# A GLA and MLP layer on one core: where prepared weight sums are made, and which steps of the output projection use them

## The chip, the cores and the metric

The kernel runs on one core of one Trainium2 chip. The metric is the device time of one execution in microseconds, the median of the runs shown; lower is better.

## The reference, cut to what matters

One layer with 256 tokens (T) of width 2048 (D): a chunk-causal gated linear attention (GLA) and a squared-ReLU MLP, each behind an RMSNorm and added to the residual, and a last RMSNorm. All is float32.

```python
h = x
h = h + _gla_mixer(_rmsnorm(h, gla_norm[j]), gla_w_in[j], gla_w_gate_up[j], gla_b_gate[j], gla_o_norm[j], gla_w_out[j])
h = h + _sq_relu_mlp(_rmsnorm(h, mlp_norm[i]), mlp_w_up[i], mlp_w_down[i])
return _rmsnorm(h, final_norm)
```

The mixer projects to q and k (1024 wide each), v and r (2048 wide each) and a gate of rank 16, attends in chunks of 64 tokens with 4 heads, normalizes each head, multiplies by silu(r) and projects back to 2048 through `gla_w_out`. The MLP goes through 8192.

## The kernel before, in words

**Splitting.** Each float32 operand is split into a high part (`hi`, rounded to fp32r by a ScalarE copy, line 123) and the rest (`lo`, a VectorE subtraction, lines 136 and 170). A product is three matmuls: high by high, low by high, high by low. Each matmul here has 128 rows, a stationary side of 128 columns and a moving side of 256. TensorE (PE) does one after the other; PEld, its weight load, runs beside it.

**Weights.** They come by DMA from SyncE's queue (SP) into one of six `raw` tiles, are split into one of five pairs of slots `hi` and `lo` (`wpool`, `slots`), and a slot is free again when PE has used it. So the loads and the splitting run ahead of PE as far as raw tiles and slots allow.

**Stages, in order of time.** v's first half with the gate (`natural`); k's two halves and then q's two halves (`turned`, 24 matmuls to a pair of k-tiles, line 224); four groups `x_group` 0 to 3 for v's second half and r's first half; r's second half (`natural`, line 181); the output projection as four groups `out_group` 0 to 3 of 512 columns; the MLP (line 1022). While the stages up to the q halves run, `pump` places small jobs of other work between their k-tiles: it takes one from `side` and one from `jobs` after each k-tile, 15 times to a half.

**Groups (`group`, line 305).** A group takes the 8 pairs of k-tiles in a written order. A *plain* pair is 8 blocks of 3 = 24 matmuls. A pair *by sums* (those in `summed`) uses seven products in place of eight, 21 matmuls, on sums and differences of the four blocks of weights and of the four blocks of the other side: 9 matmuls on the weights as they are, in the pair's own step, and 12 on the sums (`pending`), behind the next step's products. The sums are made on the spot: the load adds two blocks by a DMA from GpSimd's queue (POOL, line 335), VectorE does `weight_sums` (lines 233 and 234), ScalarE and VectorE split them again (lines 123 and 365). A step whose place is in `between` has other work behind its products.

**Prepared steps (`make_sums`, `make_all`).** For the pairs in `MADE_OUT`, as (group, pair) of the output projection, the sums are made earlier, by two jobs from `jobs`: `high` loads the weights, adds and subtracts on VectorE (lines 252, 233, 234), rounds on ScalarE (255) into a slot and writes it to HBM from POOL's queue (256); `low` subtracts (259) and writes the rest (260). The slot is held until both writes have landed. `MADE_AT` has the places, one tuple for each call of `next(make)`, a place being the number of the job in that stage. In the group, a prepared pair is loaded ready (`pre<-made`, line 330), so neither adding load, nor sums, nor their splitting is needed; only the 768 columns that the first 9 matmuls read are split.

**Two things around the change.** `xe_gt` holds copies, at another address, of the first 128 tokens of the k-tiles in `EVEN` (5 and 6). `rows_of` names pairs of an `x_group` whose first product reads its stationary side from there (`row_x`); `FIRST[2]` does that for pair 2 and also puts k-tile 5 first, `FIRST[3]` for pair 3. `two_scores` (line 697) does the attention scores of two heads, in float32, in two banks of their own and two that `x_group` 1 will use; ScalarE and VectorE evacuate them to `at` (711, 712). `turn` transposes a piece of h through PE (line 844) behind step 2 of groups 1 to 3, so that it waits for the group before to have been added up (`put`, 933).

**The order of the work.** Each engine's queue is put in order by a planner that runs a timeline of its own over the program, within what `issue_after` fixes; PE's order of products is fixed by `then_mm`. So a job that is moved can change the order on ScalarE, VectorE, POOL and SP around it.

Of the kernel before, what the change touches and what calls it, by code (L numbers as in the profile page):

```python
# [41 lines left out]
KEYW = HEADS * DK  # L42
# [6 lines left out]
GT = 512  # L49
# [20 lines left out]
def tile_gla_mlp(ctx, tc, x, xt, cols, w_vg, w_in, w_gate, w_out, w_up, w_down, final_norm, out):  # L70
# [26 lines left out]
    side, jobs = deque(), deque()  # L97
# [113 lines left out]
    def turned(row, w, c0, even=(0,), acc=None):  # L211

        acc = acc or acc_banks(GT // P // 2)
        for kp in range(KT // 2):
            wh, wl = pair_of(w, kp, c0, even)
            for i in range(2):
                kt = 2 * kp + i
                ah, al = row(kt)
                for j in range(GT // P):
                    s = slice(j * P, (j + 1) * P)  # L220
                    o = acc[j // 2][:, j % 2 * T : (j % 2 + 1) * T]
                    for n, (u, m) in enumerate(((wh, ah), (wh, al), (wl, ah))):

                        nc.tensor.matmul(  # L224
                            o, u[:, i, s], m, start=kt == 0 and n == 0 and j % 2 == 0,
                            stop=kt == KT - 1 and n == 2, skip_group_check=True,
                        )
                if kt < KT - 1:
                    pump()
        return acc  # L230
# [3 lines left out]
        return nc.vector.tensor_tensor(u[:, 1::2], u[:, 1::2], u[:, 2:3].to_broadcast([P, 2, T]), op=ALU.subtract)  # L234


    MADE_OUT = ((1, 6), (2, 1), (2, 6), (3, 1), (3, 6))
    MADE_DOWN = ()
    MADE_AT = ((0, 5, 10), (6, 10))
    made = {}  # L240

    def make_sums(key, src):

        made[key] = dram.tile([2, P, G], F32, tag=f"made{len(made)}", name="made")
        raw, to = [], []

        def high():
            raw.append(raw_tile()[:, :G])
            with tc.issue_after(last_load[0].ins):
                last_load[0] = nc.sync.dma_start(out=raw[0].rearrange("p (i c) -> p i c", i=2), in_=src)  # L250
            u = raw[0].rearrange("p (f s) -> p f s", f=4)
            nc.vector.tensor_tensor(u[:, 0], u[:, 0], u[:, 1], op=ALU.add)
            weight_sums(u)
            to.extend(slots())
            nc.scalar.copy(to[0][:, :G], raw[0])
            nc.gpsimd.dma_start(out=made[key][0], in_=to[0][:, :G].bitcast(F32))

        def low():
            nc.vector.tensor_tensor(to[1][:, :G], raw[0], to[0][:, :G].bitcast(F32), op=ALU.subtract)
            nc.gpsimd.dma_start(out=made[key][1], in_=to[1][:, :G].bitcast(F32))  # L260

        return high, low

    def make_all():
        pair = lambda w, c0, g: w[c0 : c0 + 2 * P, g * GT : (g + 1) * GT].rearrange("(i p) c -> p i c", p=P)
        todo = [make_sums((None, g, kp), pair(w_out, 2 * kp * P, g)) for g, kp in MADE_OUT]
        todo += [make_sums((ROUNDS - 1, g, kp), pair(w_down, (ROUNDS - 1) * MR + 2 * kp * P, g)) for g, kp in MADE_DOWN]
        for places in MADE_AT:
            now = [lambda: None] * (KT - 1)
            for at in places:  # L270
                now[at], now[at + 1] = todo.pop(0)
            yield now
# [155 lines left out]
    def plain_x(kt, t):  # L428
        return x_row(kt, t * P, (t + 1) * P)
# [11 lines left out]
    def from_bank(dst, bank):  # L441

        b = bank.rearrange("p (i t) -> p i t", i=2)
        nc.scalar.copy(dst[:, :, WRAP:T], b[:, :, : T - WRAP])
        nc.vector.tensor_copy(dst[:, :, :WRAP], b[:, :, T - WRAP :])
# [222 lines left out]
    def extend_q(c):  # L668
        nc.scalar.copy(qt[:, c, T : T + CHUNK], qt[:, c, CHUNK:P])
        nc.vector.tensor_tensor(  # L670
            qt[:, c, T + CHUNK :].rearrange("p (b s) -> p b s", b=2),
            qt[:, c, P:T].rearrange("p (b s) -> p b s", b=2),
            dq[:, c, :].unsqueeze(2).to_broadcast([P, 2, CHUNK]),
            op=ALU.mult,
        )

    make = make_all()
    for half in range(2):
        if half:
            jobs.extend(next(make))  # L680
        acc = turned(stream_x, w_in, half * GT, even=())
        for b in range(2):
            c0 = 4 * half + 2 * b
            from_bank(qt[:, c0 : c0 + 2], acc[b])
        side.extend([lambda c=c: extend_q(c) for c in range(4 * half, 4 * half + 4)])
# [41 lines left out]
    def two_scores(hd):  # L727
        spare = [psum_bank(i, "aux") for i in x_banks[1]]
        scores(hd)
        scores(hd + 1, spare)  # L730

    def x_group(n, c0, order, summed, between, put, rows_of={}):

        def combine(p16, p57):
            tt = nc.vector.tensor_tensor
            nc.scalar.copy(comb_x[:, 1::2], two(p16))
            nc.scalar.copy(comb_x[:, 0::2], two(p57))
            tt(comb_x[:, 3], comb_x[:, 1], comb_x[:, 3], op=ALU.add)
            tt(comb_x[:, 0], comb_x[:, 0], comb_x[:, 3], op=ALU.subtract)
            tt(comb_x[:, 3], comb_x[:, 3], comb_x[:, 2], op=ALU.add)  # L740
            tt(comb_x[:, 2], comb_x[:, 0], comb_x[:, 2], op=ALU.subtract)

        def put_all(banks):
            for t in range(NT):
                o = comb_x[:, 2 * t : 2 * t + 2]
                nc.vector.tensor_tensor(o, two(banks[t]), o, op=ALU.add)
                put(o.rearrange("p f s -> p (f s)"), t)

        def at_of(kp):
            def at(k):  # L750
                if k < A12:
                    return [x_forms[kp][:, i, k] for i in range(2)]
                t, i = divmod((A11, A12, A21, A22).index(k), 2)
                return plain_x(2 * kp + i, t)
            return at

        def row(kt, t):
            return (row_x if (kt, t) in [(2 * kp + i, t) for kp in rows_of for t, i in rows_of[kp][:1]] else plain_x)(kt, t)

        group(  # L760
            lambda kp: w_in[2 * kp * P : 2 * (kp + 1) * P, c0 : c0 + GT], [psum_bank(i) for i in x_banks[n % 2]], x_sums,
            order, summed, between, row, at_of, combine, put_all, filled=False, rows_of=rows_of,
        )

    V0 = (5, 0, 6, 2, 4, 3, 7, 1), (0, 4)
    V1 = (2, 5, 0, 3, 4, 6, 1, 7), (0, 4, 1)
    G0 = (2, 5, 0, 3, 4, 6, 1, 7), (0, 4, 1)
    G1 = (2, 0, 5, 4, 3, 1, 6, 7), (0, 4, 1)
    FIRST = {2: ((0, 1), (0, 0), (1, 0), (1, 1)), 3: ((0, 0), (0, 1), (1, 0), (1, 1))}
    rest = [side.popleft() for _ in range(len(side))]  # L770
    at_of_v = lambda c: lambda bank, t: put_v(bank, 512, t, G + c)
    x_group(0, 3 * KEYW, *V0, {
        **{i: lambda i=i: [f() for f in rest[2 * i : 2 * i + 2]] for i in range(2)},
        2: lambda: two_scores(0), 4: lambda: two_scores(2),
    }, at_of_v(0), FIRST)
    x_group(1, 3 * KEYW + GT, *V1, {}, at_of_v(GT))

    on = big.tile([P, NT, D], F32, tag="C", name="on")

# [45 lines left out]
    FORMED = (0, 1, 6, 7)  # L825
# [93 lines left out]
    def out_group(g, order, summed, between):  # L919

        def combine(p16, p57):
            tt = nc.vector.tensor_tensor
            nc.scalar.copy(comb[:, 1:3], two(p16))
            nc.scalar.copy(comb[:, 0:4:3], two(p57))
            tt(comb[:, 2], comb[:, 1], comb[:, 2], op=ALU.add)
            tt(comb[:, 0], comb[:, 0], comb[:, 2], op=ALU.subtract)
            tt(comb[:, 4], comb[:, 0], comb[:, 3], op=ALU.subtract)
            tt(comb[:, 5], comb[:, 2], comb[:, 3], op=ALU.add)

        def put(banks):  # L930
            for t in range(NT):
                o = h[:, t, g * GT : (g + 1) * GT].rearrange("p (f s) -> p f s", f=2)
                nc.vector.tensor_tensor(o, two(banks[t]), comb[:, 4 * t : 4 * t + 2], op=ALU.add)

        def at_of(kp):
            f = forms_o(kp)
            return lambda k: [a[:, k] for a in f]

        group(
            lambda kp: w_out[2 * kp * P : 2 * (kp + 1) * P, g * GT : (g + 1) * GT], [out_banks[g, t] for t in range(NT)], out_ids[4:],  # L940
            order, summed, between, row_o, at_of, combine, put, ready_of=lambda kp: made.get((None, g, kp)),
        )
# [6 lines left out]
    ORDER = (3, 0, 2, 1, 4, 7, 6, 5), (1, 3, 7, 2, 0, 6, 4, 5)  # L949
# [6 lines left out]
    hth, htl = (big.tile([P, KT, T], F32R, tag="A" + i, name="h" + i, bufs=1) for i in "hl")  # L956
    turned_h = lambda kt: [a[:, kt, :].rearrange("p (t s) -> p t s", t=NT) for a in (hth, htl)]
    for g in range(1, GROUPS):
        out_group(g, ORDER[1], FORMED, {
            2: lambda: turn(h, turned_h, g2, g - 1), 4: lambda: ssq_h(g - 1),  # L960
            **({3: lambda: begin_out(g + 1)} if g + 1 < GROUPS else {}),
        })
# [511 lines left out]
```

## Time and profile before

| what | us |
|---|---|
| runs shown | 1046.91, 1046.59, 1043.65 (median 1046.59) |
| the profiled execution | 1045.65 |
| its span, from the first to the last instruction | 1043.9 |
| PE busy | 1032.6 |
| VectorE (DVE) busy | 908.7 |
| ScalarE (ACT) busy | 755.5 |

Times in the trace count from the start of the span. A row of a timeline gives start, duration, engine, line, operation, tiles written and read, count, and in brackets the idle time of the engine just before and what ended it. A row of a window gives, for each engine, its busy time and the number of instructions that touch the window, then the granted clock of TensorE, the busy share of the DMA engines and GB/s. A row of grouped lines gives count, busy time and mean ns of one, and the idle time before. In a busy stretch of PE the matmuls overlap: each shows some 276 ns while the next starts after some 113.

### The profile page before, as it was taken

The page shows a single profiled execution, that of the slowest core. Times are in us where ns is not written, and L with a number is a line of the kernel's source. Part 1 is how long each engine was busy: PE and PEld are TensorE (multiplying, and loading weights), DVE is VectorE, ACT ScalarE, POOL GpSimd, SP SyncE. Part 2 cuts the span into 40 slices and gives each one's busy share as a digit, 9 for nine tenths or more (in the row PEclk, how much of TensorE's full clock was granted, in tenths as well). Part 3 has the DMA queues.
Part 4 walks back from the last instruction along what each step waited for, and adds up shares of the span by engine and source line. Part 5 has one row for each costly group of instructions (what it writes and reads, how often), then busy time and mean ns, then how long its engine had stood idle before and what let it go on. Part 6 is the DMA issues. An engine that isn't in the chain of part 4 may idle for free.

```text
span 1043.9 us, 23395 instructions
## 1 busy us (share of the span) xinstructions
PE 1032.6 (99%) x9013; PEld 1031.0 (99%) x9013; DVE 908.7 (87%) x1261; ACT 755.5 (72%) x1133; POOL 135.0 (13%) x183
## 2 busy tenths in 40 slices
PE   9999999999999999999999999999999999999997
PEld 9999999999999999999999999999999999999997
DVE  7768868898698866889999999999999999999887
ACT  7775456666577665677788788778778778778685
POOL 0000110220100000111111111111111111111000
PEclk9999999999999999999999999999999999999999
DMA  9866786758977987678888888888888888887772
GB/s 336 320 206 197 240 264 177 202 168 288 317 252 224 308 252 190 180 211 223 239 243 218 248 228 219 240 234 223 248 231 216 256 227 228 236 231 221 232 243 86
DMA packets 129615, 242.66 MB, mean 232 GB/s; under 512 B 11568, under 2 KB 30384, under 8 KB 129376
## 3 DMA queue, kind: packets, MB, share of 16 engines
q1 hardware_dynamic: 108048, 216.76, 66.1%
q0 software_dynamic: 20736, 22.82, 12.5%
q8 instruction: 70, 1.15, 0.4%
q10 hardware_dynamic: 720, 1.60, 0.4%
q14 instruction: 41, 0.34, 0.1%
HBM read 233.79 MB, written 7.34 MB: 231 GB/s over the span
## 4 chain that ended last, share of the span: by engine, by line
PE 94%; DVE 2%; DMA 1%; issue 1%; ACT 1%; POOL 0%; POOLq 0%; DVEq 0%; ACTq 0%
PE up L1022 33%; PE acc L1022 28%; PE acc L305 14%; PE acc L181 10%; PE acc L224 5%; PE aux L224 2%; DVE lo L136 1%; DMA made<-hi 1%; PE aux L181 1%; PE aux L844 1%; DMA raw<-in_w_in 0%; ACT hi L123 0%; PE aux L399 0%; PE aux L697 0%; DVE lo L170 0%
## 5 line engine op out<-in xcount | busy, mean ns | idle before, releaser
L123 ACT CAST hi<-raw 128x512 fp32r<-128x512 f32 (+4 forms) x656 | 518.6, 821 | 201.6 <-DVE raw L233 70.8
L136 DVE TENSOR_TENSOR lo<-raw,hi 128x768 fp32r<-128x768 f32 (+4 forms) x228 | 232.7, 1031 | 53.7 <-ACT hi L123 49.4
L1022 PE MATMUL acc<-hi,act 128*128 128x256 f32 x1696 | 247.7, 276 | 0.0
L1022 PE MATMUL up<-hh,hi 128*128 128x256 f32 x1024 | 238.7, 276 | 0.0
L1022 PE MATMUL up<-hl,hi 128*128 128x256 f32 x1024 | 238.7, 276 | 0.0
L1022 PEld LDWEIGHTS acc<-hi,act 128*128 128x128 f32 x1696 | 217.6, 188 | 0.0
L170 DVE TENSOR_TENSOR lo<-raw,hi 128x1024 fp32r<-128x1024 f32 x160 | 194.5, 1219 | 24.9 <-ACT hi L123 23.9
L1022 PEld LDWEIGHTS up<-hh,hi 128*128 128x128 f32 x1024 | 192.2, 188 | 0.0
L1022 PEld LDWEIGHTS up<-hl,hi 128*128 128x128 f32 x1024 | 192.2, 188 | 0.0
L1232 POOL DMA_DIRECT2D raw<-in_w_down x112 | 95.8, 856 | 519.8 <-DMA raw<-in_w_down 259.5
L1292 DVE TENSOR_TENSOR lo<-raw,hi 128x1024 fp32r<-128x1024 f32 x112 | 136.5, 1218 | 1.1 <-ACT hi L123 1.1
L1022 PE MATMUL up<-hh,lo 128*128 128x256 f32 x1024 | 137.0, 276 | 0.0
L1022 PE MATMUL acc<-lo,act 128*128 128x256 f32 x848 | 133.8, 276 | 0.0
L1022 PEld LDWEIGHTS up<-hh,lo 128*128 128x128 f32 x1024 | 125.7, 188 | 0.0
L1022 PEld LDWEIGHTS acc<-lo,act 128*128 128x128 f32 x848 | 113.3, 188 | 0.0
L234 DVE TENSOR_TENSOR raw<-raw 128x512 f32<-128x512 f32 x139 | 96.0, 690 | 3.5
L233 DVE TENSOR_TENSOR raw<-raw 128x256 f32<-128x256 f32 x139 | 58.8, 423 | 7.7 <-DMA raw<-in_w_out 4.7
L181 PE MATMUL acc<-hi,xA 128*128 128x256 f32 (+1 forms) x376 | 56.0, 281 | 0.0
L181 PEld LDWEIGHTS acc<-hi,xA 128*128 128x128 f32 x376 | 49.9, 190 | 0.0
L224 PE MATMUL acc<-xA,hi 128*128 128x256 f32 x288 | 49.2, 276 | 0.0
L224 PEld LDWEIGHTS acc<-xA,hi 128*128 128x128 f32 x288 | 43.4, 188 | 0.0
L1149 ACT COPY sums<-acc 128x512 f32<-128x512 f32 x46 | 26.9, 584 | 22.4 <-PE acc L1022 22.4
(226 smaller groups left out, 1450.7 us busy)
## 6 DMA issues: line engine op xcount, KB each, us to landing
raw<-in_w_up SPq DMA_DIRECT2D x128, 512.0 KB, 4.6
raw<-in_w_down SPq DMA_DIRECT2D x224, 256.0 KB, 4.4
raw<-in_w_in SPq DMA_DIRECT2D x69, 512.0 KB, 4.5
raw<-in_w_down POOLq DMA_DIRECT2D x112, 128.0 KB, 5.1
raw<-in_w_out SPq DMA_DIRECT2D x21, 512.0 KB, 6.4
raw<-in_w_down SPq DMA_DIRECT2D x16, 512.0 KB, 5.0
raw<-in_w_vg SPq DMA_DIRECT2D x14, 520.0 KB, 8.6
raw<-in_w_out SPq DMA_DIRECT2D x27, 256.0 KB, 5.3
```

Source lines behind the costliest of these rows:

```text
L123: last_hi[0] = nc.scalar.copy(to, raw)
L136: last_lo[0] = nc.vector.tensor_tensor(lo[:, s], raw[:, s], hi[:, s].bitcast(F32), op=ALU.subtract)
L170: last_lo[0] = nc.vector.tensor_tensor(to[1], dst, to[0].bitcast(F32), op=ALU.subtract)
L181: newest[0] = nc.tensor.matmul(o[:, m], x, w[:, m], start=first and c == 0, stop=last, skip_group_check=True).ins
L224: nc.tensor.matmul(o, u[:, i, s], m, start=kt == 0 and n == 0 and j % 2 == 0, stop=kt == KT - 1 and n == 2, skip_group_check=True,)
L233: nc.vector.tensor_tensor(u[:, 2], u[:, 0], u[:, 2], op=ALU.subtract)
L234: return nc.vector.tensor_tensor(u[:, 1::2], u[:, 1::2], u[:, 2:3].to_broadcast([P, 2, T]), op=ALU.subtract)
L305: newest[0] = nc.tensor.matmul(bank[:, o + d : o + d + T], x, w[:, d : d + T], start=(not filled or bank in sums_banks) and bank.name not ...
L1022: newest[0] = nc.tensor.matmul(o, x, w, start=first, stop=last, skip_group_check=True).ins
L1149: last_end[0] = nc.scalar.copy(to, src).ins
L1232: nc.gpsimd.dma_start(out=raw[:, :T], in_=src[:, 0, T:], accum_op=ALU.add)
L1292: last_lo[0] = nc.vector.tensor_tensor(to[1][:, :G], u, to[0][:, :G].bitcast(F32), op=ALU.subtract)
```

## The change

Of the output projection's prepared steps, four are left of five: pairs 1 and 6 of group 1 change places, pair 6 of group 2 is not prepared any more, pair 1 of groups 2 and 3 and pair 6 of group 3 are as before. Pair 6 of groups 1 and 2 is plain. One step is prepared in q's first half (places 2 and 3), one in its second half (4 and 5) in place of three; the two in r's second half stay. `x_group` 0 takes its pairs in another order, so that the pairs by sums, 0 and 4, are its fourth and seventh steps and no longer the second and fifth; the first two heads' scores stand behind its second step and no longer its third, the other two behind the fifth as before, and two of the four `extend_q` jobs behind the third and not the second. Pairs 2 and 3, which read `xe_gt`, stay the ones behind the scores. `x_group` 1 gets `FIRST[2]`.

```diff
-    MADE_OUT = ((1, 6), (2, 1), (2, 6), (3, 1), (3, 6))
+    MADE_OUT = ((1, 1), (2, 1), (3, 1), (3, 6))
     MADE_DOWN = ()
-    MADE_AT = ((0, 5, 10), (6, 10))
+    MADE_AT = ((2,), (4,), (6, 10))
...
     for half in range(2):
-        if half:
-            jobs.extend(next(make))
+        jobs.extend(next(make))
         acc = turned(stream_x, w_in, half * GT, even=())
...
-    V0 = (5, 0, 6, 2, 4, 3, 7, 1), (0, 4)
+    V0 = (5, 6, 2, 0, 7, 3, 4, 1), (0, 4)
...
     x_group(0, 3 * KEYW, *V0, {
-        **{i: lambda i=i: [f() for f in rest[2 * i : 2 * i + 2]] for i in range(2)},
-        2: lambda: two_scores(0), 4: lambda: two_scores(2),
+        0: lambda: [f() for f in rest[0:2]], 2: lambda: [f() for f in rest[2:4]],
+        1: lambda: two_scores(0), 4: lambda: two_scores(2),
     }, at_of_v(0), FIRST)
-    x_group(1, 3 * KEYW + GT, *V1, {}, at_of_v(GT))
+    x_group(1, 3 * KEYW + GT, *V1, {}, at_of_v(GT), {2: FIRST[2]})
...
     for g in range(1, GROUPS):
-        out_group(g, ORDER[1], FORMED, {
+        out_group(g, ORDER[1], FORMED if g == 3 else (0, 1, 7), {
             2: lambda: turn(h, turned_h, g2, g - 1), 4: lambda: ssq_h(g - 1),
```

`FORMED` is (0, 1, 6, 7), `ORDER[1]` is (1, 3, 7, 2, 0, 6, 4, 5).

## The prediction

> **What bounds the kernel now.** I read the page first, then PE in windows, then the chain of waits and the timelines around the places where PE loses time.
>
> ```profile
> span 1043.9 us, 23395 instructions
> PE 1032.6 (99%) x9013; PEld 1031.0 (99%) x9013; DVE 908.7 (87%) x1261; ACT 755.5 (72%) x1133; POOL 135.0 (13%) x183
> ```
>
> PE is busy all through. So time comes only from three things: the number of matmuls, the places where PE runs dry, and the distance between matmuls that follow each other. The page hides the third, since ends are modelled; a window shows it, by its count (columns: PE busy us, twice, count, granted clock, DMA share, GB/s):
>
> ```profile
> 161.20:191.20 30.00, 30.00 (x257) 1.00 0.68 181
> 193.00:241.00 48.00, 48.00 (x426) 1.00 0.64 181
> 327.00:339.60 12.60, 12.60 (x110) 1.00 0.97 309
> ```
>
> A window counts what overlaps its edges, so a matmul that shows 276 to 280 ns is counted 2.4 times too often. 254.6 in 30 us is one per 117.8 ns; 423.6 in 48 us is one per 113.3 ns. Both are 128x256 matmuls at clock 1.00. So there are two spacings, 4.5 ns (4%) apart; the third row (117.1) is in the long one. The long spacing starts where PE runs dry and stays. What ended it:
>
> ```profile
> 170.55 0.63 PE L305 MATMUL acc<-hi,xA 128*128 128x256 f32 x4
> ...
> 192.10 0.64 PE L305 MATMUL acc<-hi,xe_gt 128*128 128x256 f32 x4
> 192.58 0.40 PE L305 MATMUL acc<-lo,xe_gt 128*128 128x256 f32 x2
> 192.81 0.62 PE L305 MATMUL acc<-hi,xA 128*128 128x256 f32 x4
> 193.27 0.39 PE L305 MATMUL acc<-lo,xA 128*128 128x256 f32 x2
> ```
>
> The six matmuls whose stationary side is the copy xe_gt (x_group 2's first step, by FIRST[2]) stand between long and short: from 192.81 four take 0.46 us. x_group 1 lies whole in the long spacing: 183 matmuls from 170.55 to 192.10.
>
> **Dry spots in x_group 0.**
>
> ```profile
> 143.74 0.67 PE L305 MATMUL acc<-hi,xE 128*128 128x256 f32 x4
> 144.93 0.50 PE L305 MATMUL acc<-lo,xE 128*128 128x256 f32 x2 [0.52 <-DVE lo L136]
> 145.27 0.63 PE L305 MATMUL acc<-hi,xE 128*128 128x256 f32 x4
> ...
> 148.86 3.25 PE L697 MATMUL aux<-qt,kab 128*128 128x128 f32 x24
> 151.86 0.72 PE L305 MATMUL acc<-hi,xe_gt 128*128 128x256 f32 x4
> ...
> 155.72 0.28 PE L305 MATMUL acc<-lo,xf 128*128 128x256 f32 x1
> 156.39 0.92 PE L697 MATMUL aux<-qt,kab 128*128 128x192 f32 x4 [0.39 <-DVE at L712]
> 158.14 2.67 PE L697 MATMUL aux<-qt,kab 128*128 128x128 f32 x20 [0.83 <-PE aux L697]
> 160.57 0.72 PE L305 MATMUL acc<-hi,xe_gt 128*128 128x256 f32 x4
> ```
>
> At 143.74, six matmuls take 1.53 us where 6 x 0.1133 = 0.68 would do: 0.85 lost. The first scores take 3.00 us (148.86 to 151.86); the second 160.57 - 155.84 = 4.73: 1.73 lost, for the evacuations of the first (`at`, L712). Where the first loss is from:
>
> ```profile
> 134.09 8.41 DMA made<-hi
> ```
>
> ```profile
> 142.57 1.05 ACT L123 CAST hi<-raw 128x1024 fp32r<-128x1024 f32 x1 [7.05 <-DMA made<-hi]
> ```
>
> The third prepared step of the q projection's second half keeps one of five weight slots until its write has landed; ACT sits 7.05 us before it can split step 2's weights, DVE behind it. That backlog is also why the first scores are evacuated so late.
>
> **Dry spots in the output projection.**
>
> ```profile
> 315.87 1.38 PE L844 MATMUL aux<-ident,h 128*128 128x128 f32 x8
> 317.00 0.48 PE L305 MATMUL acc<-hi,oth 128*128 128x256 f32 x2
> ...
> 322.94 0.54 PE L305 MATMUL acc<-lo,oth 128*128 128x256 f32 x3
> 323.71 1.26 PE L305 MATMUL acc<-hi,of 128*128 128x256 f32 x8 [0.24 <-ACT hi L123]
> 325.50 0.74 PE L305 MATMUL acc<-lo,of 128*128 128x256 f32 x4 [0.52 <-DVE lo L365]
> ...
> 326.97 0.40 PE L305 MATMUL acc<-hi,oth 128*128 128x256 f32 x2
> ...
> 339.69 1.03 PE L844 MATMUL aux<-ident,h 128*128 128x128 f32 x8
> 340.49 0.48 PE L305 MATMUL acc<-hi,oth 128*128 128x256 f32 x2
> ```
>
> Group 1's eight transposes take 1.13 us, group 2's 0.80: 0.33 lost, waiting for h. From 322.94 to 326.97 stand 21 matmuls in 4.03 us; 2.38 would do: 1.65 lost, and the long spacing stays until the transposes at 339.69 (12.72 us, 108 matmuls, 0.49 lost). Here VectorE is the cause:
>
> ```profile
> 296.00:309.00 13.00, 13.00 (x116) 13.00 (x115) 12.72 (x17) 8.51 (x12) 0.84 (x1) 1.00 0.82 280
> 309.00:326.00 17.00, 16.12 (x134) 15.47 (x133) 15.18 (x24) 12.97 (x25) 0.86 (x1) 1.00 0.66 196
> ```
>
> ```profile
> L136 DVE TENSOR_TENSOR lo<-raw,hi 128x1024 fp32r<-128x1024 f32 x14 | 16.8, 1221 | 1.3 <-ACT hi L123 1.3
> L136 DVE TENSOR_TENSOR lo<-raw,hi 128x768 fp32r<-128x768 f32 x15 | 14.3, 953 | 0.5 <-ACT hi L123 0.5
> L365 DVE TENSOR_TENSOR lo<-raw,hi 128x1024 fp32r<-128x1024 f32 x11 | 13.4, 1222 | 3.0 <-ACT hi L123 2.9
> L234 DVE TENSOR_TENSOR raw<-raw 128x512 f32<-128x512 f32 x10 | 6.9, 689 | 0.2
> L233 DVE TENSOR_TENSOR raw<-raw 128x256 f32<-128x256 f32 x10 | 4.2, 423 | 3.6 <-DMA raw<-in_w_out 3.6
> ```
>
> In the windows of all engines the columns are PE, PEld, DVE, ACT, POOL: DVE is busy 12.72 of 13, then 15.18 of 17 us. The other rows give the pieces: a step by sums made on the spot costs DVE 0.95 + 0.42 + 0.69 + 1.22 = 3.28 us, a prepared one 0.95, a plain one 1.22.
>
> **The change, part by part.**
>
> (a) Prepared steps in the q halves. Before three in half 1, after one in each half. One costs DVE 0.42 + 0.42 + 0.69 + 1.22 = 2.75 us (L252 taken at the 0.42 of L233, same shape), ACT one 1.05 us cast, SP one load, POOL two writes, and one of five slots. Half 1 loses 5.5 us of DVE work, and its last write is issued six jobs earlier (4 for 10, one job per 12 matmuls: 8.2 us). The 0.85 at 143.74 goes. What is late next: slots stay 4 x 24 x 0.1133 = 10.9 us ahead of PE, less 2.7 for a held one, so ACT and DVE reach x_group 0 with 8 us in hand; the ends are 0 and 0.85.
>
> In half 0 the prepared step is new, and its cover must be looked at:
>
> ```profile
> 85.00:100.00 15.00, 15.00 (x135) 15.00 (x134) 14.09 (x22) 6.99 (x8) 0.00 (x0) 1.00 0.83 243
> 100.00:110.00 10.00, 10.00 (x91) 10.00 (x90) 5.84 (x10) 7.54 (x8) 0.00 (x0) 1.00 0.64 171
> ```
>
> ```profile
> 93.84 1.05 ACT L123 CAST hi<-raw 128x1024 fp32r<-128x1024 f32 x1 [1.67 <-PE acc L224]
> ```
>
> DVE has 0.9 us free in 85 to 100 and 4.2 in 100 to 110. ACT's cast at 93.84 waits for PE to free a slot, so splitting is as far ahead as slots allow: about 8.6 us (10.9 less cast and subtraction, 2.3). A held slot takes 2.7, DVE's added work 2.75: 3 us stay. POOL, which issues the writes, has nothing else there (0.00), and SP's one load meets a DMA share of 0.83, then 0.64. I take nothing; if the cover goes, PE runs dry by what is missing, bounded by the 1.73 above, and the long spacing comes early (rival 3). Below nothing it cannot be: PE is not dry there now.
>
> (b) V0's order. Both lots of scores are still followed by the xe_gt steps (kp 2, kp 3). Between the two lots lie now two plain steps, a first half and a second half of sums: 24 + 9 + 24 + 12 = 69 matmuls, some 8 us, where before were 36 (151.86 to 155.84, 4 us). The evacuation of the first scores, on ACT and DVE among casts, ended near 156.3, 4.4 us after them. I take all of the 1.73; ends 0 and 1.73, nearer to the upper since the ACT backlog goes too. The first scores come a step earlier and share banks with q's half 1; two plain steps (48 matmuls, 5.4 us) still lie between. Two extensions of q run a step later, three steps ahead of the scores that read them. Both xe_gt steps behind scores leave the long spacing as it is (161.20 row); I expect that again. Steps 0 and 1 now run at 113.3 before the scores: some 20 matmuls, 0.1.
>
> (c) V1 with FIRST[2]. Enters as x_group 2 did at 192.10, from the long spacing with the same six matmuls: 177 x 4.5 ns = 0.79 gained; x_group 2's own then costs 6 x 4.5 ns. Ends 0 and 0.82.
>
> By the Trainium skill (TensorE: Matmul & The Clock Gate, Back-to-back issue gap) a warm gap is N/2.4 + 2.5 ns, 109.2 for 256 columns, whatever tile the operand is read from; by it (c) is worth 0. The rows show 113.3 and 117.8 at the same N and clock, so the trace does not agree.
>
> (d) Group 1: pair 1 prepared, 6 plain. DVE loses 3.28 - 0.95 = 2.33 us before the transposes, and gains 0.27 for pair 6. Between pair 0's first half and its sums stand 24 matmuls, not 9: 1.7 us more time. So 3.7 us of slack against 1.65 lost: I take all of 0.33 + 1.65 + 0.49 = 2.47. The ends are 0 and 2.47. PE pays 3 matmuls, 0.34. SP's two reads of a made tile are for pair 1 and not pair 6; POOL has one adding load less:
>
> ```profile
> 292.81 2.41 SPq L330 DMA_DIRECT2D pre<-made x4
> ```
>
> The first two made tiles are read at 292.81 now, as soon as their buffers come free, and would be then, some 20 us ahead of pair 1's sums.
>
> (e) Group 2: 6 plain, not prepared: DVE +0.27, 1 MB less to load, PE 0.34. Groups 0 and 3, the r projection's two prepared steps and the MLP stay as they are.
>
> Sum: 0.85 + 1.73 + 0.10 + 0.79 + 2.47 - 0.68 = 5.26 us. The profiled execution took 1045.65 us for its span of 1043.9; it lies between the runs shown (1043.65 to 1046.91, median 1046.59). 1045.65 - 5.26 = **1040.4**.
>
> **Rivals.** (1) VectorE still late in group 1: (d) gives only its cost, 1045.65 - 3.47 + 0.68 = 1042.9. For it: 12.72 of 13 us busy in group 0, which the change leaves; against: the work that goes lies ahead of the loss. (2) The wait in x_group 0 moves and isn't removed, to the first sums or the scores' banks; the planner orders the queues anew, so the change would not do what it says: 2.68 stays, 1043.1. (3) **Slower**: the prepared step in half 0 makes PE dry. Point: a backlog of over 3 us on DVE or ACT around 100 to 110. Price: 1.7 dry, then the long spacing until 241, where the second window above ends, since the xe_gt steps behind scores have failed twice and V1's and x_group 2's would too: 136 us from 105, less the 47.2 (144.9 to 192.1) that have it now, 88.8 x 4.5/117.8 = 3.4; with (a) and (b) lost because the queues stay late, and (d) and (e) gained (1.79), 1.7 + 3.4 - 1.8 = 3.3 slower, 1049.0. (4) The spacing follows other things than the xe_gt reads: (c), 0.10 and 0.49 go, 1041.8. The skill's rule above would give this.
>
> **Numbers.** Forecast 0.60; rival 1 0.12; 2 0.12; 3 0.10; 4 0.06. The runs shown spread 2.0 below and 1.3 above the profiled one. Low end 1040.4 - 2.0 = 1038.4, rounded to 1038.0; high end rivals 1 and 2 plus 1.3, 1044.4, rounded to 1045.0; rival 3 is left out. A measurement tells 0.3%, 3.1 us, from no change. Against 1046.59 that is 1043.5: the forecast and rival 4 count as faster but for the spread, half of 1 and 2 too, the rest as the same: faster 0.74, same 0.16, slower 0.10.
>
> **What would show it.** In the changed profile: no wait of ACT for the DMA of made ahead of x_group 0 (a); PE from the second scores to the next step 3.0 us (b); 113 ns in x_group 1 (c); no idle PE ahead of `of` and transposes of 0.8 us in group 1 (d). Wrong would be: PE dry in 95 to 140, 118 ns in x_group 1, or `lo` L365 still ahead of PE in group 1.

## The result and the profile after

The changed kernel takes 1040.67 us, the median of 7 runs (1039.66 to 1042.01). The kernel before took 1045.94 on the same chip (7 runs, 1043.65 to 1048.08). The ratio is 0.9953, 95% interval 0.9938 to 0.9968: 0.5% faster, 5.27 us between the medians. The profiled execution took 1040.84 us.

First the head of the page:

```profile
span 1039.1 us, 23376 instructions
PE 1030.4 (99%) x9019; PEld 1029.5 (99%) x9019; DVE 903.5 (87%) x1254; ACT 754.1 (73%) x1130; POOL 134.4 (13%) x180
```

There are six matmuls more (9019 for 9013) in a span 4.8 us shorter: time came from dry spots and from spacing. (Behind `make_all`'s loop a line of the changed kernel has a number one lower: L696 and L843 are L697 and L844 of before.) PE's timeline shows where; first `x_group` 0 and the starts of groups 1 and 2:

```profile
145.25 3.25 PE L696 MATMUL aux<-qt,kab 128*128 128x128 f32 x24
148.25 0.72 PE L305 MATMUL acc<-hi,xe_gt 128*128 128x256 f32 x4
...
156.46 3.25 PE L696 MATMUL aux<-qt,kab 128*128 128x128 f32 x24
159.46 0.72 PE L305 MATMUL acc<-hi,xe_gt 128*128 128x256 f32 x4
...
167.67 0.64 PE L305 MATMUL acc<-hi,xe_gt 128*128 128x256 f32 x4
...
188.45 0.64 PE L305 MATMUL acc<-hi,xe_gt 128*128 128x256 f32 x4
```

No dry spot stands ahead of the scores (in the q halves and in `x_group` 0 up to them no two matmuls start more than 0.121 us apart); both lots take 3.00 us (145.25 to 148.25, 156.46 to 159.46) where the second took 4.73. `x_group` 1 goes from 167.67 to 188.45: 20.78 us for its 183 matmuls, 21.55 before. Two windows, read as in the prediction (count less 2.4), give the spacing between the second scores and `x_group` 1, and inside it:

```profile
161.20:167.60 6.40, 6.40 (x57) 6.40 (x56) 3.91 (x7) 3.29 (x5) 0.86 (x1) 1.00 0.55 133
172.00:188.00 16.00, 16.00 (x144) 16.00 (x143) 14.94 (x20) 10.18 (x13) 1.74 (x2) 1.00 0.66 186
```

6.40/54.6 is 117 ns, 16.00/141.6 is 113. Now the output projection, from the end of group 0 to the start of group 2:

```profile
301.05 0.28 PE L305 MATMUL acc<-hi,otl 128*128 128x256 f32 x1
301.21 0.74 PE L305 MATMUL acc<-lo,oth 128*128 128x256 f32 x4
301.78 0.40 PE L305 MATMUL acc<-hi,oth 128*128 128x256 f32 x2
302.02 0.40 PE L305 MATMUL acc<-hi,otl 128*128 128x256 f32 x2
302.34 0.50 PE L305 MATMUL acc<-lo,oth 128*128 128x256 f32 x2
302.68 0.40 PE L305 MATMUL acc<-hi,oth 128*128 128x256 f32 x2
...
312.58 1.29 PE L843 MATMUL aux<-ident,h 128*128 128x128 f32 x8
313.63 0.49 PE L305 MATMUL acc<-hi,oth 128*128 128x256 f32 x2
...
321.61 1.07 PE L305 MATMUL acc<-hi,of 128*128 128x256 f32 x8
322.51 0.62 PE L305 MATMUL acc<-lo,of 128*128 128x256 f32 x4
322.97 0.39 PE L305 MATMUL acc<-hi,oth 128*128 128x256 f32 x2
...
334.53 1.03 PE L843 MATMUL aux<-ident,h 128*128 128x128 f32 x8
```

Around `of` nothing is lost (eight and four matmuls from 321.61 to 322.97, 113 ns each). But group 0 has a small new dry spot: from 301.05 to 302.68 eleven matmuls take 1.63 us, 0.38 more than 11 x 0.1133; the long spacing that follows is there in before too, from 305.85. Group 1's transposes take 1.05 us, less than before (1.13) but not 0.8.

Between marks that both kernels have, in us of PE time:

| stretch (its first matmul, before and after) | before | after | difference | predicted |
|---|---|---|---|---|
| start to k's first half (49.37, 49.18) | 49.37 | 49.18 | -0.19 | 0 |
| to `x_group` 1 (170.55, 167.67) | 121.18 | 118.49 | -2.69 | -2.68 |
| `x_group` 1 (192.10, 188.45) | 21.55 | 20.78 | -0.77 | -0.79 |
| `x_group` 2 to the output projection's first group (290.87, 287.22) | 98.77 | 98.77 | 0.00 | 0 |
| group 0 (315.87, 312.58) | 25.00 | 25.36 | +0.36 | 0 |
| group 1 (339.69, 334.53) | 23.82 | 21.95 | -1.87 | -2.13 |
| group 2 (361.04, 356.22) | 21.35 | 21.69 | +0.34 | +0.34 |
| the rest, to the last matmul | 674.99 | 674.99 | 0.00 | 0 |

### The profile page after: what moved, and what is told of

The parts are those of the page before. It is cut to its first block, busy times and chain, and to the rows that moved or that the text cites. A ratio compares the mean times of both kernels' runs of the same rounds, so it can differ in the third digit from the quotient of the medians.

```text
span 1039.1 us, 23376 instructions
## 1 busy us (share of the span) xinstructions
PE 1030.4 (99%) x9019; PEld 1029.5 (99%) x9019; DVE 903.5 (87%) x1254; ACT 754.1 (73%) x1130; POOL 134.4 (13%) x180
## 4 chain that ended last, share of the span: by engine, by line
PE 99%; issue 0%; ACT 0%; DVE 0%; POOLq 0%; POOL 0%; DVEq 0%
PE up L1021 34%; PE acc L1021 28%; PE acc L305 16%; PE acc L181 10%; PE acc L224 6%; PE aux L224 2%; PE aux L181 1%; PE aux L843 1%; PE aux L696 1%; PE aux L399 0%; ACT sqf L1360 0%; PE acc L595 0%; DVE hf L1432 0%; POOLq L1469 0%; POOL rf L521 0%
## 5 line engine op out<-in xcount | busy, mean ns | idle before, releaser
L123 ACT CAST hi<-raw 128x1024 fp32r<-128x1024 f32 (+4 forms) x654 | 518.2, 822 | 201.1 <-DVE raw L233 66.4
```

Source lines behind the costliest of these rows:

```text
L123: last_hi[0] = nc.scalar.copy(to, raw)
```

## The experiments

Each edit is against the kernel named with it. Where single executions are compared, I compare such stretches of the trace, and not the whole times: runs of the kernel before alone lay between 1042.5 and 1049.5.

### Parts of the change alone

**c_first**: before, with (c) alone.

```diff
-    x_group(1, 3 * KEYW + GT, *V1, {}, at_of_v(GT))
+    x_group(1, 3 * KEYW + GT, *V1, {}, at_of_v(GT), {2: FIRST[2]})
```

> The kernel before with one edit: x_group 1 gets FIRST[2]. My theory (two spacings of matmuls; six reads of xe_gt out of steady long spacing bring the short one back): x_group 1's 183 matmuls take 20.8 us in place of 21.55, the dry spots around 144, 156, 316 and 323 to 326 us stay, total -0.8 us. Rival (the spacing follows something else): x_group 1 stays at 21.5 us, total 0.

1044.71 us (before 1047.93). PE's timeline and a window in `x_group` 1:

```profile
168.34 0.64 PE L305 MATMUL acc<-hi,xe_gt 128*128 128x256 f32 x4
...
169.05 0.64 PE L305 MATMUL acc<-hi,xA 128*128 128x256 f32 x4
```

```profile
172.00:188.00 16.00, 16.00 (x138) 16.00 (x137) 12.87 (x15) 8.17 (x10) 1.70 (x2) 1.00 0.69 180
```

The six reads of `xe_gt` are there and the long spacing stays: 16.00/135.6 is 118 ns, the group takes 21.56. So the reads alone do not bring the short spacing back. Unasked, the stretch ahead of `x_group` 1 fell from 121.18 to 119.13, though nothing was edited there: the dry spot at 144 was absent and the second scores took 3.74. ACT's row says why:

```profile
140.36 1.05 ACT L123 CAST hi<-raw 128x1024 fp32r<-128x1024 f32 x1 [4.99 <-DMA made<-hi]
```

It waited 4.99 us for the write, not 7.05. Up to `x_group` 1 every engine does the same in the same order in both kernels, and POOL issued the write at the same point (134.21, and 134.09 in before); yet it took 6.1 us to land, and 8.4 in before. So how long that write takes varies between executions, and with it the loss that (a) and (b) remove.

**a_steps**: before, with (a) alone. **b_order**: before, with (b) alone.

```diff
-    MADE_OUT = ((1, 6), (2, 1), (2, 6), (3, 1), (3, 6))
+    MADE_OUT = ((1, 6), (2, 1), (3, 1), (3, 6))
-    MADE_AT = ((0, 5, 10), (6, 10))
+    MADE_AT = ((2,), (4,), (6, 10))
...
-        if half:
-            jobs.extend(next(make))
+        jobs.extend(next(make))
```

> The kernel before with the prepared steps alone moved: one in each half of q, (1,6), (2,1), (3,1), (3,6); pair 6 of group 2 is made on the spot; order, scores and x_group 1 as before. My theory (the slot held by the third write is the cause of the dry spot at 144, and the backlog that it leaves also of most of the scores' wait): the 0.85 us at step 2 of x_group 0 go, the second scores take 3.0 to 3.5 us in place of 4.73. Rival (the scores' wait comes from the 4 us between the two lots): they still take over 4 us. Group 1's dry spots stay as before, 0.33 and 1.65; group 2 has VectorE work for one more pair and may get dry by up to 1 us.

```diff
-    V0 = (5, 0, 6, 2, 4, 3, 7, 1), (0, 4)
+    V0 = (5, 6, 2, 0, 7, 3, 4, 1), (0, 4)
...
-        **{i: lambda i=i: [f() for f in rest[2 * i : 2 * i + 2]] for i in range(2)},
-        2: lambda: two_scores(0), 4: lambda: two_scores(2),
+        0: lambda: [f() for f in rest[0:2]], 2: lambda: [f() for f in rest[2:4]],
+        1: lambda: two_scores(0), 4: lambda: two_scores(2),
```

> The kernel before with the order of x_group 0 alone: V0 and the places of the scores as after; the prepared steps, x_group 1 and the output projection as before. Theory that (a) is needed: ACT still waits some 7 us for the third write, and PE is dry by about 0.85 us in x_group 0. Rival: the 3 us of scores that now stand ahead of step 2 hide that wait, and 69 matmuls between the scores hide the evacuation: x_group 0 has no dry spot, 2.6 us gained, with ACT's wait of 7 us still in the trace.

1043.03 and 1043.47 us (before 1047.93). From k's first half to `x_group` 1: 118.40 and 118.49 us, for 121.18 before and 118.49 after. In both runs the whole loss is gone: no dry spot near 144, both lots of scores 3.00 us. (In a_steps pair 6 of group 2 is by sums made on the spot, and the group is not dry by it: 21.35 us, as in before.) In a_steps the places of the scores are those of before:

```profile
148.41 3.25 PE L696 MATMUL aux<-qt,kab 128*128 128x128 f32 x24
151.41 0.72 PE L305 MATMUL acc<-hi,xe_gt 128*128 128x256 f32 x4
...
155.38 3.25 PE L696 MATMUL aux<-qt,kab 128*128 128x128 f32 x24
158.38 0.72 PE L305 MATMUL acc<-hi,xe_gt 128*128 128x256 f32 x4
```

The 3.97 us from 151.41 to 155.38 were enough for evacuating the first scores, once ACT was not behind. In b_order ACT still waits for the write, but 1.95 us:

```profile
137.88 1.05 ACT L123 CAST hi<-raw 128x1024 fp32r<-128x1024 f32 x1 [1.95 <-DMA made<-hi]
```

Part of that is the edit's own doing. In before, the adding load for the first pair by sums of `x_group` 0 stands ahead of the third write in POOL's queue and waits 3.01 us there, so that the write is issued at 134.09, 2.7 us behind the end of its cast. With the new order that load comes at 139.07, and the write is issued 0.3 us behind its cast:

```profile
133.52 0.90 POOL L335 DMA_DIRECT2D raw<-in_w_in  x1 [3.01 <-DMA raw<-in_w_in]
```

```profile
131.86 0.53 POOL L256 DMA_DIRECT2D made<-hi  x1 [1.14 <-ACT hi L255]
```

The first row is of before, the second of b_order. The rest is the landing, 6.0 us for 8.4, which varies. So (a) by itself cures both lots of the loss. For (b) the dry spot is less sure: its one run had a fast landing, and c_first has the spot absent by chance. c_sums_last, next, had the full wait. Group 1 stayed dry in both (23.83 us), as it had to.

**c_sums_last**: c_first again, with pairs 4 and 7 changed over in `V0`, so that `x_group` 0 ends on sums directly ahead of `x_group` 1, as it does in the changed kernel and ahead of `x_group` 2. By then I supposed that the reads work behind sums, and not behind the plain products of c_first.

```diff
-    V0 = (5, 0, 6, 2, 4, 3, 7, 1), (0, 4)
+    V0 = (5, 0, 6, 2, 7, 3, 4, 1), (0, 4)
```

> The kernel before with FIRST[2] in x_group 1, as in c_first, and with pairs 4 and 7 of x_group 0 changing places, so that the second pair by sums is the seventh step, and its sums are the last products ahead of x_group 1. If the xe_gt reads end the long spacing behind sums (seven of seven so far) and not behind plain products (none of one, c_first): x_group 1 takes 20.8 us. If c_first's failure was chance: 20.8 or 21.6, either way about even. Prepared steps, scores' places and output projection as before, so their dry spots may come or not.

1044.5 us, one run (before 1044.61). The reads stand behind sums, and the spacing stays long all the same (118 ns, the group 21.56):

```profile
169.20 0.64 PE L305 MATMUL acc<-hi,xe_gt 128*128 128x256 f32 x4
```

```profile
172.00:188.00 16.00, 16.00 (x138) 16.00 (x137) 14.94 (x20) 10.20 (x13) 0.86 (x1) 1.00 0.67 187
```

That theory fell too. The run shows one thing of (b) besides: the dry spot is there, and yet the second scores take 3.00 us, with 48 matmuls between the two lots for 33. PE's row at the dry spot, and ACT's wait:

```profile
145.50 0.51 PE L305 MATMUL acc<-lo,xE 128*128 128x256 f32 x2 [0.52 <-DVE lo L136]
```

```profile
143.14 1.05 ACT L123 CAST hi<-raw 128x1024 fp32r<-128x1024 f32 x1 [7.08 <-DMA made<-hi]
```

So a longer way between the scores covers the evacuation even when ACT is held its full 7.08 us, as (b) had it; the dry spot is then left, as in before.

### The cover, taken away or pushed

**d_spot**: after, with pair 1 of group 1 made on the spot. It keeps the 24 matmuls between pair 0's first products and its sums, and gives DVE its 2.33 us of work back. The prediction had counted both as slack.

```diff
-    MADE_OUT = ((1, 1), (2, 1), (3, 1), (3, 6))
+    MADE_OUT = ((2, 1), (3, 1), (3, 6))
-    MADE_AT = ((2,), (4,), (6, 10))
+    MADE_AT = ((), (4,), (6, 10))
```

> The changed kernel with pair 1 of group 1 made on the spot (three prepared steps, none in q's first half); pair 6 of groups 1 and 2 plain as in the change. If the 24 matmuls of a plain pair 6 between pair 0's two halves are what covers VectorE's lateness (1.7 us against 1.65): the dry spot at pair 0 is at most 0.3 us, the transposes still wait 0.2 to 0.4 us. If VectorE's 2.3 us that the prepared pair 1 saves are what counts: over 1 us dry at pair 0, and the transposes wait more than in the changed kernel. x_group 0 and 1 as after.

1044.14 us (before 1047.93). Group 1 is dry again: transposes 1.14 us, the group 23.86 for 21.95.

```profile
320.87 0.39 PE L305 MATMUL acc<-hi,otl 128*128 128x256 f32 x2
322.21 0.51 PE L305 MATMUL acc<-lo,oth 128*128 128x256 f32 x2 [0.95 <-DVE lo L136]
```

The wait has moved from `of` to the plain pair ahead of it: two matmuls that start 1.34 us before the next, 1.1 lost. The 24 matmuls do not cover DVE; its saved work does. The other 1.9 us of this run are a chance stall near 203 us, told below.

**f_three**: after, with three prepared steps in q's first half and none in its second.

```diff
-    MADE_AT = ((2,), (4,), (6, 10))
+    MADE_AT = ((0, 5, 10), (), (10,))
```

> The changed kernel with three of its four prepared steps in q's first half, at places 0, 5 and 10, none in the second and one in r's second half. Rival 3 (no cover in q's first half): PE dry between 95 and 145 us, with the long spacing behind it, 2 to 4 us lost. My theory: VectorE is behind by up to 3 x 2.75 us over 22 us there, PE is dry at most for some tenths; r's second half has 1.5 MB less traffic, so group 0's dry spot (0.35 us at 301 to 302 after the change) goes.

1042.76 us (before 1049.47). This is rival 3's mechanism, with three steps in place of one:

```profile
113.36 0.50 PE L224 MATMUL acc<-xE,hi 128*128 128x256 f32 x3
114.20 0.38 PE L224 MATMUL acc<-xE,lo 128*128 128x256 f32 x1 [0.34 <-DVE lo L170]
114.42 0.40 PE L224 MATMUL acc<-xE,hi 128*128 128x256 f32 x2
```

```profile
116.00:144.00 28.00, 28.00 (x240) 28.00 (x240) 21.35 (x40) 14.54 (x23) 4.10 (x18) 1.00 0.90 287
```

Four matmuls take 1.06 us (0.61 lost), and then the spacing is 28.00/237.6, 118 ns, to the scores. From k's first half to `x_group` 1 it takes 120.09 us for 118.49. One step in this half costs nothing, three cost 1.6.

**e_both**: after, with pair 6 of group 1 by sums too, prepared in q's first half: a second prepared step there, and 3 matmuls less.

```diff
-    MADE_OUT = ((1, 1), (2, 1), (3, 1), (3, 6))
+    MADE_OUT = ((1, 1), (1, 6), (2, 1), (3, 1), (3, 6))
-    MADE_AT = ((2,), (4,), (6, 10))
+    MADE_AT = ((2, 8), (4,), (6, 10))
...
-        out_group(g, ORDER[1], FORMED if g == 3 else (0, 1, 7), {
+        out_group(g, ORDER[1], (0, 1, 7) if g == 2 else FORMED, {
```

> The changed kernel with pair 6 of group 1 by sums and prepared too (five prepared steps, the second of q's first half at place 8). PE has 3 matmuls less in group 1, -0.34 us. If q's first half has the cover that I took (3 us for one step), a second one 6 jobs later leaves it covered: no dry PE between 95 and 145 us. Rival 3 of the prediction: PE gets dry there and keeps the long spacing to x_group 1, 2 us or more lost. In group 1 only 9 matmuls stand between pair 0's halves again: if VectorE's saved time is enough by itself, no dry spot at pair 0.

1040.38 us (before 1049.47). The q halves stay without a dry spot, 118.49 us to `x_group` 1; group 1 takes 21.38 us with transposes of 0.81. The three kernels below with the change's own group 1 (g_second, h_first_v, i_run) have transposes of 0.79 and take 21.69: 0.31 for three matmuls, as step (d) had priced them (0.34). A second step fits in q's first half. And only 9 matmuls stand between pair 0's halves here: VectorE's saved work covers `of` without the 24 of a plain pair.

### What ends the long spacing

**g_second**: after, with the reads of `xe_gt` as a pair's second product, six matmuls behind scores or group start.

```diff
-rows_of[kp][:1]
+rows_of[kp][1:2]
...
-    FIRST = {2: ((0, 1), (0, 0), (1, 0), (1, 1)), 3: ((0, 0), (0, 1), (1, 0), (1, 1))}
+    FIRST = {2: ((0, 0), (0, 1), (1, 0), (1, 1)), 3: ((0, 1), (0, 0), (1, 0), (1, 1))}
```

> The changed kernel with the xe_gt reads as the second product of the steps of pairs 2 and 3, behind six ordinary matmuls, and not as the first. Theory A (the xe_gt reads end the long spacing wherever six of them follow steady long spacing): the spacing is short from some 150 us on, behind the first scores, and again behind the second, 0.5 us gained. Theory B (they end it only right behind the products of a pair by sums, as x_group 1 and 2 had it, and not behind plain products, as in c_first): the long spacing stays through x_groups 1, 2 and 3 up to r's second half, about 0.8 + 2.0 us lost.

1040.83 us (before 1049.47). Behind the first scores the long spacing stays; behind the second it ends, some 8 us sooner than in after:

```profile
162.00:166.00 4.00, 4.00 (x38) 4.00 (x37) 2.23 (x4) 2.09 (x3) 0.86 (x1) 1.00 0.40 136
```

4.00/35.6 is 112 ns where after has 117. It is worth 0.22 us (118.27 to `x_group` 1 for 118.49). Neither theory had one place cured and the other not.

**h_first_v** and **i_run**: after, with the reads of one k-tile in v's first half, which lies in the long spacing; in i_run that step's matmuls are chained as well, so that nine reads follow one another.

```diff
-    acc = natural(plain_x, rows(w_vg, 0, WMAX), WMAX, cuts, ahead=input_tile)
+    acc = natural(lambda kt, t: (row_x if kt == EVEN[0] else plain_x)(kt, t), rows(w_vg, 0, WMAX), WMAX, cuts, ahead=input_tile)
```

> The changed kernel with k-tile 5 of v's first half read from xe_gt for its first 128 tokens (12 matmuls, 3 of them with 272 columns). PE has the long spacing from 5 to 62 us now. If twelve such reads end it: short from about 22 us, (62 - 22) x 4% = 1.5 us gained before k's first half ends. If they end it only behind sums: nothing, 0. If the earlier need leaves PE dry there: a loss of up to 1 us.

> The changed kernel with k-tile 5 of v's first half read from xe_gt for its first 128 tokens, as in h_first_v, and with that step's matmuls in written order, so that nine such reads stand in a row; in h_first_v they stood in threes. If a run of six or more is what ends the long spacing: short from about 22 us to 49, 27 us x 4% = 1.0 us gained before k's first half, and another 0.4 until 60. If it depends on what stands ahead: 0.

h_first_v: 1040.96 us (before 1049.47); the reads stood in runs of three and of six among matmuls of 272 columns (not in threes alone, as the expectation for i_run has it), and matmuls 100 to 384 took 34.07 us for 34.09. i_run: median 1041.0 of 6 runs, ratio to before 0.9971 (0.9959 to 0.9983); after nine reads the next nine matmuls start 113 ns apart, then 272-column reads of `xe_gt` follow, and the long spacing is back: 34.05 us.

**j_all**: e_both, g_second and i_run in one.

> All that helped, together: the changed kernel with pair 6 of group 1 by sums and prepared (e_both, -0.31 us), the xe_gt reads as second products (g_second, -0.25 us) and the run of nine in v's first half (i_run). Against the changed kernel's profile -0.6 us without an effect of the run of nine, -2.0 with it; no new dry spot in q's first half. Against the kernel before a ratio of 0.993 to 0.995.

Median 1040.03 of 5 runs, ratio 0.9963 (0.9950 to 0.9976), before 1044.61 on that chip. Its profiled execution, 1042.02, had the stall near 203 us, and group 1's transposes took 1.53 us there.

**k_nine**: j_all, with the 272-column matmuls of that step on the ordinary copy.

```diff
-lambda kt, t: (row_x if kt == EVEN[0] else plain_x)(kt, t)
+lambda kt, t: (row_x if chain[0] == 1 else plain_x)(kt, t)
```

> The kernel after with pair 6 of group 1 made by sums and pair 1 prepared, the xe_gt reads behind the second scores as the second product, and nine matmuls of 256 columns in a row from xe_gt in one step of v's first half; the 272-column matmuls of that step read the ordinary copy. Nothing of the result is left out. If it is 272-column reads of xe_gt that bring the long spacing back (in i_run three of them followed the nine), the short spacing holds from about 20 us to the next stall: the step from matmul 100 to 384 takes about 32.7 to 33.0 us for 34.07, and against the kernel before the ratio is near 0.993. If 272-column matmuls of any operand bring it back, those 284 matmuls stay at 34.0 to 34.1 us and the ratio is near 0.9955, as the same kernel without the nine in a row would have it. A chance stall near 203 us, seen in two profiles, would add 1.9 us to its profiled execution under either.

Median 1039.45 of 5 runs (1039.39 to 1040.20), before 1045.5, ratio 0.9938 (0.9922 to 0.9954). PE's timeline around the nine reads:

```profile
19.83 0.52 PE L184 MATMUL acc<-hi,xe_gt 128*128 128x256 f32 x3
...
20.90 0.50 PE L184 MATMUL acc<-hi,xA 128*128 128x256 f32 x3
21.24 0.50 PE L184 MATMUL acc<-lo,xA 128*128 128x256 f32 x3
...
22.04 0.29 PE L184 MATMUL acc<-lo,xA 128*128 128x272 f32 x1
...
23.02 0.52 PE L184 MATMUL acc<-lo,xA 128*128 128x256 f32 x3
23.37 0.87 PE L184 MATMUL acc<-hi,xA 128*128 128x256 f32 x6
```

From 20.90 three matmuls take 0.34 us; behind the 272-column ones, from 23.02, three take 0.35: long again, now with the ordinary copy. Matmuls 100 to 384 took 34.03 us. So it is 272-column matmuls, and not only reads of `xe_gt`, behind which the long spacing comes back in v's first half, as far as one place in three runs (i_run, j_all, k_nine) shows, and this part gains nothing. What k_nine and j_all gain over the change is 0.31 (three matmuls) and 0.22 (the second scores); in k_nine's trace 0.35 is lost again at group 3's transposes (1.14 us for 0.79). Against the kernel before, k_nine's interval overlaps the change's own (0.9938 to 0.9968): that it is faster than the change is not shown by the times.

## Why the prediction was right, point by point

The forecast of 1040.4 held: 1040.67 measured. The total was 5.26; the profiled executions, to which its terms belong, are 4.81 apart. That it meets the 5.27 between the medians to a hundredth is luck: single runs of the kernel before spread over 7 us, and the loss that (a) and (b) remove swings by 2. Not every step under the total held.

**(a) and (b), 0.85 + 1.73 + 0.10.** The sum held (2.69 for 2.68), the way it was put together did not. I gave the dry spot to (a) and the scores to (b), as two losses with a cure each. Both come from ACT's wait for the write of a prepared step: a_steps removes the whole without (b). The working says so itself, "that backlog is also why the first scores are evacuated so late", and then charges the scores to (b), whose own cure is real (c_sums_last) but comes second. Beside (a), (b) took nothing off this stretch (118.40 with (a) alone, 118.49 with both: the first scores, and the long spacing behind them, come 21 matmuls sooner). The 36 matmuls counted between the two lots are 33 in the trace, and the write leaves 14.7 us sooner (119.37 for 134.09) and not 8.2, in part because of the adding load ahead of it in POOL's queue, which the working did not see. c_first shows that the loss itself swings by 2 us between executions (119.13 for 121.18).

**(a), half 0 at nothing.** Held: no dry spot, and e_both fits a second step. f_three has the limit between two and three, and shows rival 3's form, dry and then the long spacing; its price there was 1.6 us, less than my 5.1 (1.7 and 3.4), since the stall lost 0.61 and the long spacing, from 114 on, did not last until 241: the reads behind the second scores ended it at 162, which I had ruled out from two cases.

**(c), 0.79.** The number held (0.77), the premise failed: "enters as `x_group` 2 did". With the same six reads c_first and c_sums_last got nothing. At group starts in the long spacing, the six reads ended it in 10 of 12 cases over all the traces, the failures being these two; in the changed kernel's own order they did so in 5 of 5. Directly behind scores they ended it in 2 of 22. I had one case (192.10) for and two against, and should have put (c) at even odds; that the number came out is in part luck. The rival by the Trainium skill's warm gap (TensorE: Matmul & The Clock Gate, Back-to-back issue gap; the page gives the formula for an isolated matmul, which these are not) fell: no trace has 109.2 ns, all have 113.3 or 117.8.

**(d), 2.47 less 0.34.** Group 1 took 1.87 less for 2.13. The missing 0.26 are the transposes, 1.05 for 0.79. They wait for h to be added up by VectorE, and that wait is not surely gone: they take 0.79 to 0.81 in e_both, g_second, h_first_v, i_run and k_nine, but 1.10 in f_three and 1.53 in j_all. In g_second, h_first_v and i_run group 1 takes 21.69: with 23.82 before, the 2.13 of the prediction. Of the two parts of the slack, d_spot shows that 2.33 us of DVE work decided and "1.7 us more time" from the 24 matmuls did not: without the first the group is dry by a like amount, one step earlier.

**(e), 0.34.** Held to the hundredth. By a_steps it need not have been paid: its group 2, with pair 6 by sums made on the spot, is not dry.

**What I didn't foresee**: 0.36 lost in group 0, which the change leaves alone. In the other eight kernels made from the changed one the group takes 24.6 to 25.0, so it is no part of the change's price; kernels made from the one before lost there too, c_first 1.30 (26.30), b_order 0.26, c_sums_last 0.20. In the changed kernel DVE sat idle for 3.17 us until 280.52, some 7 us ahead of the group, for a load with adding:

```profile
280.52 0.43 DVE L233 TENSOR_TENSOR raw<-raw 128x256 f32<-128x256 f32 x1 [3.17 <-DMA raw<-in_w_out]
```

The traces bear out that this wait is the cause. DVE waited 3.01 us there in c_sums_last, 3.08 in b_order, 3.17 in the changed kernel and 4.10 in c_first, and the loss in group 0 was 0.20, 0.26, 0.36 and 1.30: each time the wait less 2.8. In the ten other traces the wait was 2.55 us or less, and the group was not dry. No run set the wait on purpose.

## What to carry to other kernels

When two losses stand a few microseconds apart on one engine, ask first whether one late queue feeds both, and price the cures together: running each edit alone told what the sum could not. Cover is counted in the engine that is late (its work ahead of the due time), not in matmuls between two marks. Before a wait is priced from one execution, look at how far the transfer behind it varies; here one write's landing moved 2 us.

## What the runs showed of the hardware

**Two lasting spacings.** 128x256 matmuls with a weight load each start 113.3 or 117.8 ns apart at granted clock 1.00. A stall of PE of some 0.02 us can be enough to leave the short one (g_second and i_run in group 0, one interval of 117 or 118 ns and one of 124 there; in j_all one of 126 was not). Then two things were seen to end it. One is transposes: in 21 of 21 cases in which the spacing ahead of them was long (groups 1 and 2, and near 250 us in d_spot and j_all), it was short again 10 to 12 matmuls behind them. The other is a run of reads from the copy at another address, which itself takes some 119 ns a matmul. (Near 62.8 us every trace turns short with neither.) From the short spacing such a run never brought the long one. From the long one it depends on something finer: at group starts six reads worked in 10 of 12 cases, in v's first half nine worked in 3 of 3, behind the first scores as second product six worked in 0 of 3, behind the second in 3 of 3. At group starts the six intervals were 118, 119, 121, 117, 117, 121 ns where after's `x_group` 1 turned short, and 117, 118, 119, 121, 117, 118 where c_first's did not. The pattern looks like the same one a place later, so the phase in which the reads begin may decide. What sets it stays open.

**A stall by chance.** Two of 14 profiled executions (d_spot, j_all) lost 1.93 us between 203 and 250 us (from `x_group` 2 to the output projection 100.69 us for 98.77 in all others). In d_spot's timelines:

```profile
197.59 0.85 POOL L335 DMA_DIRECT2D raw<-in_w_in  x1 [6.65 <-DVE oss L792]
198.15 1.59 POOL L521 TENSOR_TENSOR ors<-oss,mhalf 128x1 f32<-128x1 f32 x1
200.72 1.30 POOL L521 TENSOR_TENSOR ors<-oss,mhalf 128x1 f32<-128x1 f32 x1 [0.98 <-DVE oss L792]
```

```profile
202.06 0.81 DVE L795 TENSOR_SCALAR on<-aux,r1k,ors 128x512 f32<-128x512 f32 x1 [0.44 <-POOL ors L521]
202.75 0.28 PE L305 MATMUL acc<-lo,xf 128*128 128x256 f32 x1
203.01 0.47 PE L181 MATMUL aux<-vh,at 128*128 128x256 f32 x2
```

POOL's operation on one column takes 1.59 and 1.30 us where after shows 0.93 and 0.55 for it:

```profile
196.63 0.86 POOL L335 DMA_DIRECT2D raw<-in_w_in  x1 [5.82 <-DMA raw<-in_w_in]
197.54 0.93 POOL L521 TENSOR_TENSOR ors<-oss,mhalf 128x1 f32<-128x1 f32 x1
200.05 0.55 POOL L521 TENSOR_TENSOR ors<-oss,mhalf 128x1 f32<-128x1 f32 x1 [1.58 <-DVE oss L792]
```

So POOL's two operations start 0.6 us later in d_spot, and each takes some 0.7 us longer. DVE is then late with `on` (till 202.87), PE's next use of `aux` starts 0.26 us after the matmul before it for 0.11, and the long spacing that follows costs the rest. Why they are longer stays open. The load with adding issued just ahead does not explain it: after has one there too (196.63), and its operation at 221.10 takes 1.40 us with no issue in the 10 us before.
